# Output weights and residual rows of a dilated-attention layer prepared ahead, in the stage of the values

## The chip, the cores and the metric

One of the eight cores of a Trainium2 chip runs the kernel. The metric is the device time of one execution in microseconds (us); the time of a version is the median of its runs. Engines are named as the profile names them: PE (TensorE), DVE (VectorE), ACT (ScalarE), POOL (GpSimd) and SP (SyncE), whose queue issues most transfers.

## The reference

Two post-norm layers over x of 1024 rows by 1024 columns, in f32. Each sub-layer is modulated by a conditioning vector c, and its residual is scaled by ALPHA:

```python
for i in range(DEPTH):                       # DEPTH = 2
    shift, scale, gate = ada_mod(c, ada_w[i, 0], ada_b[i, 0])
    h = x * (1.0 + scale) + shift
    y = mixer_a(h, ...) if i % 2 == 0 else mixer_b(h, b_w_qkv, b_w_out, slopes)
    x = layer_norm(ALPHA * x + gate * y, ln_g[i, 0], ln_b[i, 0])
    shift, scale, gate = ada_mod(c, ada_w[i, 1], ada_b[i, 1])
    h = x * (1.0 + scale) + shift
    y = squared_relu_mlp(h, mlp_w_up[i], mlp_w_down[i])
    x = layer_norm(ALPHA * x + gate * y, ln_g[i, 1], ln_b[i, 1])
```

The change lies in `mixer_b`, the attention of the second layer. h times `b_w_qkv` gives query, key and value of 16 heads for each of three patterns (dilation 1, 4 and 16). Each pattern attends within its window, the three outputs are weighted by the softmax of their log-sum-exps and added, and the sum (1024 by 1024) is multiplied by `b_w_out`. The result, times `gate`, is added to ALPHA times the normalised rows of the sub-layer before, which are (z - mean) * rstd * ln_g + ln_b.

## The kernel before

Every f32 product is made of three products of rounded halves: a tensor is split into `hi` (a cast, on ACT) and `lo` (the rest, on DVE), and hi*hi, hi*lo and lo*hi are summed in PSUM. `split` (lines 102 and 103) is the helper for it, so that nearly all splits have these two lines; the tile's name tells them apart. Stages follow one another: `mixer_a` (gMLP), `mlp(1)`, `values`, `attention` with its tail `go_on`, `mlp(3)`. Tile pools give buffers by tag; an instruction that writes a buffer again waits for its last reader. A scheduler orders each engine's instructions when the kernel is built, except those pinned by `keep_in_program_order`.

**`values`** (line 1131 on) makes the values of the three patterns and the queries and keys of the first. A 1024 by 1024 by 1024 product is done by seven products of half-size blocks instead of eight (a Strassen scheme); `V_STEPS` lists five such groups of seven steps, numbered p = 1, 2, 5, 6, 7, 4, 3. A step (a block product) is four row blocks m of 12 matmuls, 48 in all. While step n runs, its loop loads the raw right-hand blocks of step n+2 (`vraw`, `v_r`, `v_t`, from SP), splits those of step n+1 into `vrhi` and `vrlo`, and evicts its own sums: p = 1, 5 and 6 by a copy on ACT (`vpart`), the others by an addition and a split into `vs` or `qs`, which a DMA of POOL's queue stores to DRAM. Some steps continue a sum in the PSUM bank of an earlier one (1, 6, 7, 4 in one, 2 and 5, 3 in others), so an eviction has to be done before the bank's next step. The left-hand forms are built on the way by a generator (`stream`); the four tiles `l21` are held until the last group, where they are split again (`place("L21", ...)`).

**`attention`** works through 24 groups, eight head pairs `hp` of three patterns g each. `order` and `slots` lay its steps out by hand: a group has eight slots of two halves, and `at(slot, half)` puts a step there. Meanwhile `project()` makes queries and keys of the other patterns, and fills PE between the small matmuls of the groups. Per group `scores` and `soften` give the probabilities `p`, `transposes` turns them (`pT`), `halve` splits them (`pThi`, `pTlo`), `weighted` multiplies them with the values (`pv`, line 1527), and `gather` copies the sum (`oT`, lines 1536 and 1537). `merge` joins the three patterns of a pair: it reads the statistics (`mst`), computes weights (`ma`), writes them to DRAM (`w_dram`), reads them back spread over all rows (`bc`, line 1611), scales `oT` by them (line 1623), adds (line 1627) and cuts the result (`oTs`, or `o_dram` for the first six pairs). Its twelve steps begin 18 half-slots after the pair's base.

Two more jobs lie in the slots. The **residual rows**: the affine part of the layer norm before (times ln_g, plus ln_b, both scaled by ALPHA) is applied to the eight row blocks of `spill[1]`, in slots 0 to 23 (`affine_load`, `affine_row`, line 1678); the first output rows add them by a DMA. The **output weights**: `staged_unit` loads 128 rows of `b_w_out` (`wo_raw`), multiplies them by the gate (line 1712) and splits them (`wo_hi`, `wo_lo`): units 0 to 3 from 14 slots before the last group on, 4 and 5 within it, 6 and 7 at its end and in `go_on`. `accumulate` (line 1756) makes the output product from them in five parts, named in the sums: `psoa`, `psob` between the last groups, then, behind the last `pv`, `psoc`, `psod` and `psoe` in `go_on` and beside the start of `mlp(3)`.

Of the kernel before, what the change touches and what calls it, by code (L numbers as in the profile page):

```python
# [10 lines left out]
F32 = mybir.dt.float32  # L11
# [24 lines left out]
def trunk(ctx: ExitStack, tc: tile.TileContext, x, c, ada_w, ada_b, ln_g, ln_b, a_w_in, a_b_in,  # L36
# [165 lines left out]
    def run(gen):  # L202
        for _ in gen:
            pass
# [867 lines left out]
    v_dram = [dram.tile([S, N_PAIRS, 4 * HEAD], F32, name=f"v_{g}") for g in range(3)]  # L1072

    qk_dram = dram.tile([N_PAIRS, 2, P, 2, S], F32, name="qk_0")

    class RightForms:
        BLOCK = {1: (0, 0), 2: (1, 0), 5: (0, 1), 6: (1, 1), 7: (0, 1), 4: (1, 0)}
# [53 lines left out]
    def values(before, right, ahead):  # L1131
# [3 lines left out]
        with ExitStack() as ph:  # L1135
# [12 lines left out]
            def x_tile(nm):  # L1148
                return xp.tile([P, HALF], F32, name=nm, tag="x")

            l21 = [hold.tile([P, HALF], F32, name=f"l21_{k}") for k in range(4)]

            def h_row(k, dst):
                pst = bank("tr", f"pst_2_0_{k}")
# [18 lines left out]
            def second():  # L1173

                for f in ("L22", "S1"):
                    form[f] = form_tile(f)
                for f in ("S2", "S3"):
                    form[f] = form_tile(f, act2)
                form["S4"] = form_tile("S4", top)
                x22 = []  # L1180
                for k in range(4):
                    h_row(k, l21[k][:])
# [3 lines left out]
                    V.tensor_tensor(s1[:], l21[k][:], x22[k][:], op=ALU.add)  # L1186
                    place("S1", k, s1[:])
                    yield
                trs.close()
                open_psum(trs, "VX", pbx=2)  # L1190
                built.add("S1")
                for k in range(4):
                    s3 = x_tile(f"s3_{k}")
                    sub(s3[:], form["L11"][:, 0, k, :], l21[k][:])
                    plus_lo("L11", k, s3[:])
                    place("L22", k, x22[k][:])
                    sub(x22[k][:], x22[k][:], s3[:])
                    place("S2", k, x22[k][:])
                    yield
                    place("S3", k, s3[:])  # L1200
                    yield
                built.add("S2")
                built.update(("S3", "L22"))
                for k in range(4):
                    s4 = x22[k]
                    sub(s4[:], form["L12"][:, 0, k, :], s4[:])
# [8 lines left out]
            def evict(g, X, p, m):  # L1215
# [10 lines left out]
                if X < 2:  # L1226
# [7 lines left out]
                nc.gpsimd.dma_start(v_dram[g][i * P : (i + 1) * P, 4 * dh : 4 * dh + 4, :],  # L1234
                                  v[:].rearrange("p h f c -> p h (f c)").bitcast(F32))

            for n, (g, X, p) in enumerate(V_STEPS):
                while name[p] not in built:
                    next(stream)
                for m in range(4):  # L1240
                    if m % 2 == 0 and n + 1 < len(V_STEPS):
                        right.prepare(*V_STEPS[n + 1], m // 2)
                    if m % 2 and n + 2 < len(V_STEPS):
                        right.load(*V_STEPS[n + 2], m // 2)
                    if p in (1, 2, 5):
                        kind = "pa" if p == 1 else "pbx" if m > 1 and n > 1 else "pb"
                        sums["pa" if p == 1 else "pb", m] = bank(kind, f"psv{p}_{g}_{X}_{m}")
                    acc = sums["pb" if p in (2, 5, 3) else "pa", m][:]
                    left = form[name[p]]
                    for kp in range(2):  # L1250
                        r = right.ready[g, X, p, kp]
                        for k in range(2):
                            for a, b in TERMS:
                                rows, cols_ = left[:, a, 2 * kp + k], r[b][:, k]
                                if X < 2:
                                    rows, cols_ = r[a][:, k], left[:, b, 2 * kp + k]
                                T.matmul(acc, rows[:, m * P : (m + 1) * P], cols_,  # L1257
                                         start=p in (1, 2, 5) and kp + k + a + b == 0,
                                         stop=kp == 1 and k == 1 and a == 1, skip_group_check=True)
# [12 lines left out]
    def attention(form):  # L1272
# [5 lines left out]
        with ExitStack() as ph:  # L1278
# [290 lines left out]
            def merge(hp, oTs):  # L1569
# [74 lines left out]
                steps = [lambda f=f, g=g, half=half: f(g, half) for f, g in pieces for half in range(2)]  # L1644
                pace = 2 if hp < N_PAIRS - 2 else 1
                for n, f in enumerate(steps):
                    n = pace * n + 18
                    at(base + n // 2, n % 2)(f)

            for hp in range(N_PAIRS):  # L1650
# [7 lines left out]
                merge(hp, oTs)  # L1658


            affine = {}

            def affine_load(i):
                if i == 0:
                    for n, src in (("g", ln_g), ("b", ln_b)):
                        affine[n] = row_bc(f"aff_{n}")
                        nc.sync.dma_start(affine[n][:], src[0, 1].partition_broadcast(P))
                t = affine[i] = vec.tile([P, S], F32, name=f"aff_{i}", tag="oT", bufs=4) if i < 4 else row_bc(f"aff_{i}")
                nc.sync.dma_start(t[:], spill[1][i * P : (i + 1) * P, :])

            def affine_scale():
                for n in "gb":
                    A.mul(affine[n][:], affine[n][:], ALPHA)

            def affine_row(i):
                t = affine[i]
                for n, op in (("g", ALU.mult), ("b", ALU.add)):
                    tc.keep_in_program_order(V.tensor_tensor(t[:], t[:], affine[n][:], op=op))
                nc.gpsimd.dma_start(spill[1][i * P : (i + 1) * P, :], t[:])

            at(0, 0)(affine_scale)
            for i in range(NT):
                if i > 3:
                    at(5 * i - 15, 0)(lambda i=i: affine_load(i))
                at(*((i + 1, 1) if i < 4 else (5 * i - 12, 1)))(lambda i=i: affine_row(i))
# [7 lines left out]
            def pinned_split(hi, lo, src):  # L1693
                for x_ in split(hi, lo, src):
                    tc.keep_in_program_order(x_)

            @at(last_group - 13, 0)
            def gate_row():
                ending["gate"] = vec.tile([P, D], F32, name="gate_2", tag="oT", bufs=4)
                nc.sync.dma_start(ending["gate"][:], gate_dram[2].partition_broadcast(P))  # L1700

            def staged_unit(k, load, gate, ready):
                box = {}

                @at(last_group + load[0], load[1])
                def load_raw():
                    box["raw"] = wts.tile([P, D], F32, name=f"wo_{k}_raw", tag="raw", bufs=2)
                    nc.sync.dma_start(box["raw"][:], b_w_out[0, k * P : (k + 1) * P, :])

                @at(last_group + gate[0], gate[1])  # L1710
                def apply_gate():
                    tc.keep_in_program_order(V.tensor_tensor(box["raw"][:], box["raw"][:], ending["gate"][:], op=ALU.mult))

                def split_raw():
                    hi, lo = (wts.tile([P, D], F32R, name=f"wo_{k}_{m}", tag=f"w{m}")[:] for m in ("hi", "lo"))
                    pinned_split(hi, lo, box["raw"][:])
                    ending["units"][k] = hi, lo

                if ready is None:
                    return split_raw  # L1720
                at(last_group + ready[0], ready[1])(split_raw)

            staged_unit(0, (-14, 0), (-12, 0), (-11, 0))
            staged_unit(1, (-13, 0), (-11, 1), (-10, 1))
            staged_unit(2, (-11, 0), (-10, 0), (-9, 0))
            staged_unit(3, (-10, 1), (-9, 1), (-8, 0))
            staged_unit(4, (-2, 0), (2, 0), (8, 0))
            staged_unit(5, (-1, 0), (4, 0), (8, 1))
            late = [staged_unit(6, (9, 0), (11, 1), None), staged_unit(7, (9, 1), (12, 1), None)]

            @at(last_group - 9, 0)
            def rows_first():
# [45 lines left out]
            def go_on():  # L1778
                steps = ending["merge"]
                for n, _ in enumerate(accumulate(1, range(2, 4), name="c")):  # L1780
                    if n > 4:
                        steps.pop(0)()
                for f in late:
                    f()
# [13 lines left out]
            lead, credit = 7 * KD, 0  # L1798
            for n in range(lead):
                next(stream)  # L1800
                if 16 <= n < 20:
                    affine_load(n - 16)
            due = 0
            for n, slot in enumerate(slots):
                for half, pos in enumerate(slot):
# [52 lines left out]
```

## Time and profile before

| what | us |
|---|---|
| median of 3 runs (lowest to highest) | 2732.57 (2730.59 to 2736.09) |
| the profiled execution, its own time | 2727.96 |
| its span in the profile | 2726.2 |
| `values`, in the span | 991 to 1377 |
| `attention` to the last `pv` | 1377 to 2033 |
| `psoc`, `psod`, `psoe` | 2033 to 2096 |
| `mlp(3)`, the rest | 2096 to 2726 |

Times in the profile count from the start of the span. A row of a group reads: line, engine, operation, output <- inputs, shapes and count | busy time in us, mean of one in ns | idle time of the engine just before it, and what ended most of it. A row of a wait reads: who waited <- for whom: us in total, times, the longest. A row of the timeline begins with its start and length in us.

### The profile page before, as it was taken

Reading aid. Unit: us, or ns where it says so; the run is one execution under the profiler, and the core shown is the slowest. Engines: PE = TensorE matmul, PEld = TensorE weight load, DVE = VectorE, ACT = ScalarE, POOL = GpSimd, SP = SyncE. Lnnn points to the kernel's source line nnn. Section 1 sums busy time; section 2 is a strip of 40 time slices with the busy share of each in tenths; the row PEclk is TensorE's granted clock in tenths of the full one; section 3 lists DMA queues with packets and bytes.
Section 4 is the critical chain, followed back from the end, with each engine's and each line's share of the span. In section 5 each row is a group of like instructions: output and inputs, shape, how many; then the busy total and the mean of one; then the engine's idle time right before and its main releaser. Section 6 shows DMA issues by size and latency. Waiting matters only on the chain.

```text
span 2726.2 us, 36911 instructions
## 1 busy us (share of the span) xinstructions
PE 2658.8 (98%) x13242; PEld 2196.3 (81%) x13242; DVE 1989.8 (73%) x3594; ACT 1377.1 (51%) x2593; POOL 97.0 (4%) x161
## 2 busy tenths in 40 slices
PE   6999999999999999999999999999999999999998
PEld 5788888887888878888888888888777788878886
DVE  6787698787867778555557767777768966577877
ACT  3354375555443464434436666666655655554332
POOL 1000000000000000111110000000010000000000
PEclk9999999999999999999999999999999999999999
DMA  7534346667936545655565554555672654485562
GB/s 263 159 118 134 116 140 224 227 214 257 333 131 194 195 155 193 212 186 182 178 210 153 155 140 129 132 144 139 193 183 105 202 189 159 149 311 192 171 207 86
DMA packets 332572, 487.98 MB, mean 179 GB/s; under 512 B 50988, under 2 KB 176340, under 8 KB 332388
## 3 DMA queue, kind: packets, MB, share of 16 engines
q1 hardware_dynamic: 318564, 435.29, 50.3%
q0 software_dynamic: 13824, 50.34, 5.2%
q8 instruction: 104, 1.70, 0.3%
q14 instruction: 80, 0.66, 0.1%
HBM read 357.01 MB, written 128.53 MB: 178 GB/s over the span
## 4 chain that ended last, share of the span: by engine, by line
PE 77%; DVE 12%; DMA 6%; ACT 3%; issue 2%; SPq 1%; DVEq 0%; ACTq 0%
PE psd L955 22%; PE psv L1257 13%; PE psua L796 7%; PE psq L1358 6%; PE psk L1358 6%; DMA adaw<-in_ada_w_dram 3%; PE psuc L796 3%; PE psd_wout L389 3%; PE psu L368 3%; PE pv L1527 3%; PE sc L1447 2%; PE psv L470 2%; PE psub L796 2%; DVE adaacc L128 1%; DVE left L103 1%
## 5 line engine op out<-in xcount | busy, mean ns | idle before, releaser
L796 PE MATMUL psua<-right,left 128*128 128x512 f32 x1536 | 363.4, 390 | 0.3
L955 PE MATMUL psd<-rhi,lhi 128*128 128x512 f32 x896 | 349.9, 390 | 3.0 <-ACT part L827 3.0
L955 PE MATMUL psd<-rlo,lhi 128*128 128x512 f32 x896 | 349.6, 390 | 0.2
L955 PE MATMUL psd<-rhi,llo 128*128 128x512 f32 x896 | 349.2, 390 | 0.0
L796 PEld LDWEIGHTS psua<-right,left 128*128 128x128 f32 x1536 | 287.1, 188 | 61.7 <-DVE right L103 1.4
L1469 ACT ACTIVATE p<-p,stat 128x128 f32<-128x128 f32 (+1 forms) x384 | 168.7, 441 | 107.8 <-DVE stat L1467 104.7
L955 PEld LDWEIGHTS psd<-rhi,lhi 128*128 128x128 f32 x896 | 168.6, 188 | 39.1 <-ACT part L827 3.9
L955 PEld LDWEIGHTS psd<-rlo,lhi 128*128 128x128 f32 x896 | 168.5, 188 | 35.9 <-DVE rlo L103 1.1
L955 PEld LDWEIGHTS psd<-rhi,llo 128*128 128x128 f32 x896 | 168.6, 188 | 35.0
L796 PE MATMUL psuc<-right,left 128*128 128x512 f32 x768 | 187.2, 390 | 0.0
L128 DVE SCALAR_TENSOR_TENSOR adaacc<-adaw,silu_c,adaacc 128x512 f32<-128x512 f32 x168 | 128.5, 775 | 55.0 <-DMA adaw<-in_ada_w_dram 54.6
L796 PEld LDWEIGHTS psuc<-right,left 128*128 128x128 f32 x768 | 143.5, 188 | 30.0 <-DVE right L103 0.4
L103 DVE TENSOR_TENSOR pTlo<-pT,pThi 128x512 fp32r<-128x512 f32 (+1 forms) x160 | 99.3, 621 | 75.1 <-ACT pThi L102 74.1
L103 DVE TENSOR_TENSOR left<-ws,left 128x512 fp32r<-128x512 f32 x128 | 87.8, 688 | 71.5 <-ACT left L102 69.7
L103 DVE TENSOR_TENSOR llo<-lraw,lhi 128x1024 fp32r<-128x1024 f32 x112 | 136.4, 1218 | 0.8 <-ACT lhi L102 0.8
L102 ACT CAST left<-ws 128x512 fp32r<-128x512 f32 x128 | 79.1, 620 | 99.1 <-DVE ws L717 87.8
L1358 PE MATMUL psk<-form_L,wqk_hi 128*128 128x512 f32 x384 | 127.0, 412 | 0.0
L1358 PE MATMUL psq<-form_L,wqk_hi 128*128 128x512 f32 x384 | 126.4, 410 | 0.0
L102 ACT CAST rhi<-rraw 128x1024 fp32r<-128x1024 f32 x48 | 50.6, 1053 | 139.6 <-issue 113.7
L1257 PE MATMUL psv<-vrhi,form_S 128*128 128x512 f32 x384 | 119.9, 390 | 0.6 <-ACT vrhi L102 0.4
L102 ACT CAST lhi<-lraw 128x1024 fp32r<-128x1024 f32 x112 | 117.4, 1048 | 3.5 <-PE psua L796 3.5
L1467 DVE CUSTOM_DVE_ANT_0 p<-sc,bias 128x128 f32<-128x128 f32 (+1 forms) x384 | 113.6, 346 | 6.7 <-PE sc L1447 5.8
(326 smaller groups left out, 6094.4 us busy)
## 6 DMA issues: line engine op xcount, KB each, us to landing
lraw<-forms SPq DMA_DIRECT2D x112, 512.0 KB
adaw<-in_ada_w_dram SPq DMA_DIRECT2D x192, 256.0 KB
up<-in_mlp_w_up_dram SPq DMA_DIRECT2D x64, 512.0 KB
forms<-s SPq DMA_DIRECT2D x128, 256.0 KB
rraw<-in_mlp_w_down_dram SPq DMA_DIRECT2D x64, 512.0 KB
forms<-part SPq DMA_DIRECT2D x96, 256.0 KB
v<-vs POOLq DMA_DIRECT2D x48, 512.0 KB, 3.7
vraw<-in_b_w_qkv_dram SPq DMA_DIRECT2D x42, 512.0 KB
```

The source lines that it names most:

```text
L102: first = A.copy(hi, src) if hi_engine is A else hi_engine.tensor_copy(hi, src)
L103: return first, lo_engine.tensor_tensor(lo, src, hi, op=ALU.subtract)
L128: ins = V.scalar_tensor_tensor(acc[:], raw[:], silu_c[:, k : k + 1], acc[:], ALU.mult, ALU.add)
L368: T.matmul(dst, s[a], m[b], start=(n == 0), stop=(n == last))
L389: T.matmul(p[:], stat[a][:, k, o : o + P], u[b][:, w], start=n == 0, stop=n == count - 1)
L796: T.matmul(acc, w[:, a, k, :], right[p][:, b, k, :], start=p in (1, 2, 5) and k + a + b == 0, stop=k == 3 and a == 1, skip_group_check=True)
L955: ins = T.matmul(sums[kind, m][:], l[a][:, k, m * P : (m + 1) * P], r[b][:, k, :], start=p in (1, 5, 2, 3) and kp + k + a + b == 0, stop=k ...
L1257: T.matmul(acc, rows[:, m * P : (m + 1) * P], cols_, start=p in (1, 2, 5) and kp + k + a + b == 0, stop=kp == 1 and k == 1 and a == 1, ski ...
L1358: T.matmul(p[:], wu[a][:, k * P : (k + 1) * P], h_op(k, half, b), start=k + c_ == 0, stop=k == KD - 1 and c_ == 2)
L1467: V.tensor_tensor_reduce(out=pr, in0=banks[e][:, sl], in1=st["bias"][:, width - w :], scale=-0.125, scalar=3e38, op0=ALU.add, op1=ALU.min, ...
L1469: A.activation(pr, pr, AF.Exp, bias=nm, scale=-1.0, accum_out=l)
L1527: T.matmul(pvs[b][:, q0 % HALF : q0 % HALF + w_], stt, x_[:, o_ : o_ + w_], start=not begun[b], stop=left[b] == 0, skip_group_check=True)
```

## The change

Both jobs move into `values`, as 24 pieces. The four `l21` tiles become two tiles of twice the size under one tag (`side`, two buffers); once the forms are built they are stored to DRAM by POOL (`x21_dram`), and the two buffers serve the pieces. From the sixth step on, each step begins one piece (its load, from SP) and carries out the one before it: sixteen weight pieces (half a unit each: load, times gate, split, store to `wo_dram`) and eight row pieces (256 rows of half the columns: load, times g, plus b, store back to `spill[1]`). No piece begins in the first four steps of the last group, in which `l21` is read back into the two buffers. In `attention` both jobs go; a unit is now two loads of 512 KB, hi and lo, each issued where a tile comes free: unit 3 into the two `raw` tiles, units 0, 1, 2 and 4 into `whi` and `wlo` behind the last project units, 7 into a tile of the values, 5 and 6 behind units 0 and 1. The twelve steps of a merge begin 22 half-slots after the base instead of 18.

```diff
-            l21 = [hold.tile([P, HALF], F32, name=f"l21_{k}") for k in range(4)]
+            side = [hold.tile([P, 2, HALF], F32, name=f"l21_{k}", tag="side", bufs=2) for k in range(2)]
+            l21 = [side[k // 2][:, k % 2, :] for k in range(4)]
...
+                for k in range(2):
+                    nc.gpsimd.dma_start(x21_dram[k], side[k][:])
                 built.add("S2")
...
+            def row_halves(*srcs):
+                across.clear()
+                for src in srcs:
+                    across.append(work.tile([P, HALF], F32, name=f"row_{len(across)}", tag="h"))
+                    nc.sync.dma_start(across[-1][:], src.partition_broadcast(P))
+
+            def weight_piece(k, dh):
+                if k + dh == 0:
+                    row_halves(gate_dram[2, 0:HALF], gate_dram[2, HALF:])
+                t = side_tile(f"wo_{k}_{dh}")
+                nc.sync.dma_start(t[:, 1], b_w_out[0, k * P : (k + 1) * P, dh * HALF : (dh + 1) * HALF])
+                yield
+                V.tensor_tensor(t[:, 1], t[:, 1], across[dh][:], op=ALU.mult)
+                split(t[:, 0].bitcast(F32R), t[:, 1].bitcast(F32R), t[:, 1])
+                nc.gpsimd.dma_start(wo_dram[k, :, dh, :, :], t[:])
+
+            def row_piece(i, dh):
+                w = slice(dh * HALF, (dh + 1) * HALF)
+                if i == 0:
+                    row_halves(ln_g[0, 1, w], ln_b[0, 1, w])
+                t = side_tile(f"aff_{i}_{dh}")
+                src = spill[1][2 * i * P : 2 * (i + 1) * P, w].rearrange("(n p) c -> p n c", p=P)
+                nc.sync.dma_start(t[:], src)
+                yield
+                if i == 0:
+                    for r in across:
+                        A.mul(r[:], r[:], ALPHA)
+                for n in range(2):
+                    V.tensor_tensor(t[:, n], t[:, n], across[0][:], op=ALU.mult)
+                    V.tensor_tensor(t[:, n], t[:, n], across[1][:], op=ALU.add)
+                nc.gpsimd.dma_start(src, t[:])
+
+            pieces = deque([weight_piece(k, dh) for k in range(N_PAIRS) for dh in range(2)] + [row_piece(i, dh) for dh in range(2) for i in range(4)])
...
                     evict(g, X, p, m)
+                    if n > 4 and m == 0:
+                        for _ in range(len(begun)):
+                            next(begun.popleft(), None)
+                        if pieces and n not in (28, 29, 30, 31):
+                            begun.append(pieces.popleft())
+                            next(begun[-1])
...
-                        place("L21", m, l21[m][:])
+                        place("L21", m, back[m // 2][:, m % 2, :])
+                    if (g, X) == V_STEPS[-1][:2] and p == 2 and m < 2:
+                        back.append(side_tile(f"back_{m}"))
+                        nc.sync.dma_start(back[m][:], x21_dram[m])
...
-                    n = pace * n + 18
+                    n = pace * n + 22
...
-            affine = {}
...
-            staged_unit(0, (-14, 0), (-12, 0), (-11, 0))
...
+            def load_unit(k):
+                if k == 7:
+                    t = qp.tile([P, 2, D], F32R, name="wo_7", tag="v")
+                    ending["units"][k] = tuple(t[:, i, :] for i in range(2))
+                else:
+                    ending["units"][k] = tuple(wts.tile([P, D], F32R, name=f"wo_{k}_{m}", tag="raw" if k == 3 else f"w{m}", bufs=2 if k == 3 else 4)[:] for m in ("hi", "lo"))
+                for i, t in enumerate(ending["units"][k]):
+                    nc.sync.dma_start(t.rearrange("p (d c) -> p d c", c=HALF).bitcast(F32), wo_dram[k, :, :, i, :])
+
+            for k, half_slot in ((3, -34), (0, -32), (1, -30), (2, -27), (4, -15), (7, 11), (5, 17), (6, 18)):
+                in_half(2 * last_group + half_slot, 4)(lambda k=k: load_unit(k))
```

More of the change, by code (lines that the diff above doesn't have):

```diff
@@ L1074, in trunk @@
     qk_dram = dram.tile([N_PAIRS, 2, P, 2, S], F32, name="qk_0")
+    wo_dram = dram.tile([N_PAIRS, P, 2, 2, HALF], F32, name="wo_parts")
+    x21_dram = dram.tile([2, P, 2, HALF], F32, name="x21")
     class RightForms:
@@ L1181, in second @@
                 for k in range(4):
-                    h_row(k, l21[k][:])
+                    h_row(k, l21[k])
                     x22.append(x_tile(f"l22_{k}"))
@@ L1185, in second @@
                     s1 = work.tile([P, HALF], F32, name=f"s1_{k}", tag="h")
-                    V.tensor_tensor(s1[:], l21[k][:], x22[k][:], op=ALU.add)
+                    V.tensor_tensor(s1[:], l21[k], x22[k][:], op=ALU.add)
                     place("S1", k, s1[:])
@@ L1193, in second @@
                     s3 = x_tile(f"s3_{k}")
-                    sub(s3[:], form["L11"][:, 0, k, :], l21[k][:])
+                    sub(s3[:], form["L11"][:, 0, k, :], l21[k])
                     plus_lo("L11", k, s3[:])
@@ L1235, in evict, with side_tile @@
                                   v[:].rearrange("p h f c -> p h (f c)").bitcast(F32))
+            back, across, begun = [], [], deque()
+            def side_tile(nm):
+                return hold.tile([P, 2, HALF], F32, name=nm, tag="side", bufs=2)
+            def row_halves(*srcs):
[28 more added lines that the diff above has]
+            pieces = deque([weight_piece(k, dh) for k in range(N_PAIRS) for dh in range(2)] + [row_piece(i, dh) for dh in range(2) for i in range(4)])
             for n, (g, X, p) in enumerate(V_STEPS):
+                if n == 5:
+                    run(stream)
                 while name[p] not in built:
@@ L1658, in attention @@
                 merge(hp, oTs)
-            affine = {}
[L1663 to L1685, printed above, removed]
             last_group = 8 * (len(order) - 1)
@@ L1691, in attention @@
             done = ending["res"] = Residual(2)
[L1693 to L1721, printed above, removed]
@@ L1723, in attention @@
-            staged_unit(0, (-14, 0), (-12, 0), (-11, 0))
[L1724 to L1729, printed above, removed]
+            def load_unit(k):
[6 more added lines that the diff above has]
+                    nc.sync.dma_start(t.rearrange("p (d c) -> p d c", c=HALF).bitcast(F32), wo_dram[k, :, :, i, :])
@@ L1782, in go_on @@
                         steps.pop(0)()
-                for f in late:
-                    f()
                 for f in steps:
@@ L1800, in attention @@
                 next(stream)
-                if 16 <= n < 20:
-                    affine_load(n - 16)
             due = 0
```

## The prediction

> **What bounds the kernel now.** I read the page's head first, then a table of stretches cut by stage, then who PE and VectorE waited for, and last the instructions of VectorE and PE in the one stretch that is bad.
>
> ```profile
> span 2726.2 us, 36911 instructions
> PE 2658.8 (98%) x13242; PEld 2196.3 (81%) x13242; DVE 1989.8 (73%) x3594; ACT 1377.1 (51%) x2593; POOL 97.0 (4%) x161
> ```
>
> PE is busy almost throughout, so an edit on another engine pays only where PE stands idle or runs at a reduced clock. The table of stretches says where that is (the number behind POOL's is the granted clock, then come the DMA share and GB/s).
>
> ```profile
> core 0: us, PE busy (x) PEld busy (x) DVE busy (x) ACT busy (x) POOL busy (x), PEclk, DMA share, GB/s
> 991.00:1377.00 386.00, 385.36 (x1714) 318.24 (x1713) 248.09 (x311) 171.65 (x244) 47.83 (x80) 1.00 0.57 197
> 1410.00:1500.00 90.00, 89.88 (x601) 75.01 (x600) 64.82 (x175) 54.28 (x161) 9.84 (x13) 1.00 0.48 141
> 1500.00:1700.00 200.00, 196.96 (x1316) 164.50 (x1315) 142.54 (x444) 126.30 (x379) 5.95 (x16) 1.00 0.53 142
> 1700.00:1950.00 250.00, 249.98 (x1702) 211.20 (x1703) 175.44 (x559) 159.34 (x480) 7.24 (x20) 1.00 0.52 142
> 1950.00:1960.00 10.00, 9.51 (x66) 7.98 (x64) 8.48 (x21) 6.68 (x18) 0.81 (x2) 1.00 0.75 219
> 1960.00:1970.00 10.00, 6.25 (x47) 5.30 (x46) 7.00 (x22) 5.41 (x20) 0.00 (x0) 0.96 1.00 308
> 1970.00:1980.00 10.00, 7.35 (x44) 5.53 (x42) 10.00 (x16) 4.60 (x9) 0.00 (x0) 0.84 0.76 244
> 1980.00:1990.00 10.00, 10.00 (x43) 8.29 (x43) 5.09 (x18) 6.67 (x20) 2.50 (x4) 0.85 1.06 269
> 2020.00:2030.00 10.00, 8.84 (x59) 7.60 (x58) 6.55 (x18) 7.21 (x13) 1.71 (x2) 1.00 0.64 103
> 2030.00:2040.00 10.00, 8.96 (x29) 7.20 (x30) 8.01 (x13) 1.52 (x3) 0.00 (x0) 0.66 0.71 189
> ```
>
> The first row is the values stage, into which the change moves work: PE idles 0.64 us of 386, VectorE has 138 us free, DMA runs at 0.57. The second is the start of attention, out of which the residual rows are taken: PE idles 0.12 us there. Idle PE lies at 1500 to 1700 (3.04 us), 1950 to 1980 (0.49 + 3.75 + 2.65 = 6.89 us) and 2020 to 2040 (1.16 + 1.04 = 2.20 us). Besides that the clock falls: ten microseconds at 0.96, 0.84, 0.85 and 0.66 are 0.4 + 1.6 + 1.5 + 3.4 = 6.9 us of lost time, all behind those two idle stretches. What PE waited for, from 1410 to 1950 and then from 1950 to 2040:
>
> ```profile
> PE pv L1527 <- DVE pTlo L103: 2.7, 4, 1.2
> PE pv L1527 <- ACT pThi L102: 0.3, 1, 0.3
> ...
> PE pv L1527 <- DVE pTlo L103: 4.9, 6, 2.3
> PE pv L1527 <- ACT pThi L102: 3.7, 2, 3.3
> ```
>
> It is always the split of a transposed probability tile, so VectorE (or ScalarE behind it) was late. Of VectorE's own waits in 1410 to 1950 one group matters, and the timeline shows the bad stretch:
>
> ```profile
> DVE bc L1623 <- DMA bc<-w_dram: 14.2, 5, 3.7
> ...
> 1963.92 1.98 DVE L1623 TENSOR_TENSOR bc<-oT,bc 128x512 f32<-128x512 f32 x2 [1.97 <-DMA bc<-w_dram]
> 1969.09 1.21 DVE L1712 TENSOR_TENSOR wo_raw<-wo_raw,gate 128x1024 f32<-128x1024 f32 x1
> 1978.70 1.21 DVE L103 TENSOR_TENSOR wo_lo<-wo_raw,wo_hi 128x1024 fp32r<-128x1024 f32 x1
> ...
> 1967.71 0.33 PE L1527 MATMUL pv<-pThi,v 128*128 128x128 f32 x1 [3.26 <-ACT pThi L102]
> 1978.22 0.33 PE L1527 MATMUL pv<-pTlo,v 128*128 128x128 f32 x1 [2.27 <-DVE pTlo L103]
> ```
>
> VectorE takes its queue in order. The merge's scaling (L1623) waits for the spread weights `bc` to land, and the splits behind it wait too; then gate products and splits of the output weights, 1.2 us each, stand before the next splits.
>
> **The change part by part.** Removed from attention:
>
> ```profile
> L1712 DVE TENSOR_TENSOR wo_raw<-wo_raw,gate 128x1024 f32<-128x1024 f32 x8 | 9.7, 1218 | 0.7 <-DMA wo_raw<-in_b_w_out_dram 0.6
> L103 DVE TENSOR_TENSOR wo_lo<-wo_raw,wo_hi 128x1024 fp32r<-128x1024 f32 x8 | 9.6, 1215 | 0.5 <-ACT wo_hi L102 0.4
> L1678 DVE TENSOR_TENSOR aff<-aff,aff_b 128x1024 f32<-128x1024 f32 x8 | 9.9, 1240 | 0.2
> L1678 DVE TENSOR_TENSOR aff<-aff,aff_g 128x1024 f32<-128x1024 f32 x8 | 9.8, 1219 | 0.0
> ```
>
> *Residual rows* (16 x 1.23 = 19.7 us of VectorE at 1410 to 1500). PE idles 0.12 us there: gain 0.
>
> *Merge steps two slots later* (18 to 22 half-slots). Some 200 slots lie between the first scores and the first product that follows the last group:
>
> ```profile
> 1415.29 1.48 PE sc L1447 x24
> ...
> 2032.97 13.16 PE psoc L1756 x48
> ```
>
> A slot is thus 3.1 us (estimate), and the scaling comes 6.2 us later. The longest wait for `bc` is 3.7 us, so every one ends before the scaling asks. PE's waits in this stretch are 3.0 us, not all of them behind `bc`: gain 2.5 us (0 to 3.0). Late next are the end of the merge and the store of its rows, which are read only in the output product.
>
> *Gate products and splits* (16 x 1.22 = 19.4 us of VectorE). The same two groups in 1950 to 1980 alone:
>
> ```profile
> L1712 DVE TENSOR_TENSOR wo_raw<-wo_raw,gate 128x1024 f32<-128x1024 f32 x4 | 4.9, 1213 | 0.0
> L103 DVE TENSOR_TENSOR wo_lo<-wo_raw,wo_hi 128x1024 fp32r<-128x1024 f32 x4 | 4.8, 1210 | 0.4 <-ACT wo_hi L102 0.4
> ```
>
> That is 9.7 us where VectorE is full. With them and the wait for `bc` gone, of the 6.89 us I take 6.0 (bounds 3 and 6.9): the merge of the seventh head pair still falls into this stretch, though 6 us later, where VectorE was half idle (5.09 of 10). The two dips of the clock behind it go as well: 3.5 us (0 to 3.5).
>
> The Trainium skill (TensorE: Matmul & The Clock Gate, Part 1) says that the clock is halved after an idle window of about 3.4 us and given back after a busy one. The largest single gap here, 3.26 us, agrees, but the later dips follow gaps of 2.27 us and less, so by that rule taken strictly only the first dip (0.4 + 1.6 = 2.0 us at most) would go with the gap, and the sum would be 3.2 us smaller. The measured windows decide.
>
> *Last group*, 2020 to 2040. Two splits of output weights stand in front of the last probability splits:
>
> ```profile
> 2030.33 1.22 DVE L103 TENSOR_TENSOR wo_lo<-wo_raw,wo_hi 128x1024 fp32r<-128x1024 f32 x1
> 2030.47 0.39 PE L1527 MATMUL pv<-pTlo,v 128*128 128x256 f32 x1 [0.95 <-DVE pTlo L103]
> ```
>
> They go, but this stretch is also a bare chain of transpose, split, product with nothing to fill it, so I take half: 1.1 of 2.2 us idle, 1.7 of 3.4 us clock (bounds 0 and 5.6).
>
> *Unit loads.* Sixteen loads of 512 KB replace eight and the gate row: about 4 MB more on SP's queue. Each waits for its tile (last project units, then the second half's first product). Queued behind them are `mst`, `w_dram` and `bc` of the last two merges. Units 0 to 3 go out before the tail, as tiles come free, where DMA stands at 0.52; cost 0, up to the whole 6.9 us if `bc` is pushed behind them (second rival).
>
> **What the values stage pays.** Its rows for 512 columns, a block product, and the transfers:
>
> ```profile
> L1223 DVE TENSOR_TENSOR vpart<-psv,vpart 128x512 f32<-128x512 f32 x60 | 41.1, 685 | 6.3 <-PE psv L1257 6.3
> L103 DVE TENSOR_TENSOR vs<-vpart,vs 128x512 fp32r<-128x512 f32 x36 | 24.8, 688 | 11.0 <-ACT vs L102 11.0
> L102 ACT CAST vs<-vpart 128x512 fp32r<-128x512 f32 x36 | 22.4, 621 | 55.7 <-DVE vpart L1223 28.5 <-DMA v<-vs 19.0 <-DVE vraw L1110 4.6
> ...
> 1377.21 10.88 PE psq L1358 x48
> 2155.67 4.18 DMA adaw<-in_ada_w_dram
> ...
> adaw<-in_ada_w_dram SPq DMA_DIRECT2D x192, 256.0 KB
> v<-vs POOLq DMA_DIRECT2D x48, 512.0 KB, 3.7
> ```
>
> Sixteen weight pieces cost VectorE 16 x (0.685 + 0.688) = 22.0 us, eight row pieces 8 x 4 x 0.685 = 21.9 us: 44 us into 138 us free. Over 29 products of 48 matmuls (10.88 us) that is 1.5 us a product. DMA gets 16 x 0.75 MB + 8 x 1 MB = 20 MB over 316 us, 63 GB/s on 197; the row at 1960 shows 308 GB/s at share 1.00, so it fits on average. Raw blocks for the products and the stores of `v` share the two queues with the pieces: SP waits for a side tile's store before it can issue a piece's load, and raw blocks stand behind.
>
> In the built order VectorE gets about six weight pieces between the last split for product 6 and the third eviction of product 7, three turns of each tile, with PE-critical splits between them. A turn by rows is load 4.18 + 0.685 + 0.621 + 0.688 + store 3.7 = 9.9 us, perhaps 10.5 with hand-overs (estimate). From product 5's middle to the point where product 4 needs that eviction's bank are 3.1 products, 34 us: three turns of 10.5 just fit. I take 2.5 us of PE idle for the stage. Bounds: not below -0.6 (PE idles no more than that now), and 44 us were all of it on the path; I stay near the lower end because an eviction's bank is asked for one product less one block later, 10.88 - 2.72 = 8.2 us.
>
> The Trainium skill (DMA: Bandwidth & Descriptors, Anatomy of one DMA) gives 2.0 us plus bytes over 436 KB per us; that makes 2.6 us for the load and 3.2 us for the store, an estimated turn of 7.8 us, by which the stage would pay nothing and the sum would be 2.5 us better. The store's row is 3.7 us, so I keep the rows.
>
> **Sum.** 2.5 + 6.0 + 3.5 + 1.1 + 1.7 - 2.5 = 12.3 us less. The profiled execution took 2727.96 us (span 2726.2 and 1.8 around it), 4.6 us under the median of the runs; I take the difference from the median: 2732.6 - 12.3 = 2720.3 us.
>
> **Rivals.**
>
> *The two tiles turn too slowly (slower than before).* In the values stage a VectorE instruction of a piece waits for a load that waits for a store, and splits and evictions wait behind it. For: the queue order above, and ScalarE already waits 19.0 us for stores of `v` in the row quoted. Against: the 8.2 us of cover. It decides from a turn of about 12.4 us, where 3 x (3 x 1.1 + 1.7) is 15. Three turns fit until 34 / 3 = 11.3 us. At 13.5 us they overrun by 6.6 us in each of the three groups of products that take pieces, and each such idle stretch brings a dip of 1.7 us as above: 3 x 8.3 = 25 us against 14.8 gained, about 2743 us.
>
> *The wait for `bc` stays* (no measurable change). With 4 MB more in flight at a share near 1.00, the last two spreads land later by as much as the merge was put back. Then 1950 to 1990 keep their idle time and dips, and only the early merges and the last group gain: 2.5 + 2.8 - 2.5 = 2.8 us, about 2730 us. Against: loads leave early.
>
> *The work removed was not what held PE*: the splits are late because of ScalarE (3.7 of the 8.6 us are laid at `pThi`). Then half of 1950 to 1980 remains: half of its dips too: 12.3 - 3.0 - 1.8 = 7.5 us, about 2725 us, still faster.
>
> **How the numbers follow.** Differences under 0.2% (5.5 us) can't be told from none. Forecast with its weaker form (third rival): 0.68, all faster. `bc` stays: 0.13, same. Slow turn: 0.19, slower. Low end: all bounds, 3.0 + 6.9 + 3.5 + 5.6 = 19.0 us, and 1.5 of scatter give 2712. High end: 2737, which takes in the second rival and the milder part of the first, and leaves out its worse part.
>
> **What would show it.** Right: PE idle of under 1.5 us and the clock at 1.00 in the stretches that answer to 1950 to 1990; no wait of VectorE for `bc` in the early merges; the values stage at 386 to 390 us with PE idle of 1 to 4 us. Wrong: PE waits for `vrlo`, `vrhi` or `vpart` in the values stage of over 8 us with dips of the clock there; or `bc` still ending VectorE's idle time before L1623's successor, with DMA near 1.00; or the dip after the last group unchanged.

## The result, and the profile after

The changed kernel takes **2751.09 us** (median of 6 runs, 2749.04 to 2757.96) against 2730.99 us for the kernel before (6 runs, 2725.82 to 2736.09): a ratio of 1.0079, 95% interval 1.0062 to 1.0095. It is 20 us slower where 12 us less had been forecast. The head of the profile after:

```profile
span 2749.1 us, 37080 instructions
PE 2664.9 (97%) x13242; PEld 2198.7 (80%) x13242; DVE 1993.0 (72%) x3626; ACT 1377.2 (50%) x2603; POOL 105.2 (4%) x179
```

VectorE's work is what it was (1989.8 us before), and PE's, for the same number of products, has grown by 6 us, so most of the difference is waiting. Stage by stage, from the starts of TensorE's first and last products of each stage in the two traces:

| stretch | before | after | difference |
|---|---|---|---|
| values, first to last `psv` | 385.6 | 417.0 | +31.4 |
| first `sc` to first `psoc` | 617.5 | 610.9 | -6.6 |
| `psoc` to the first product of the next MLP | 62.9 | 61.0 | -1.9 |
| from there to the end | 620.0 | 620.2 | +0.2 |

What the change was to win behind the values stage is there, at 8.5 us instead of 14.8. The whole loss is in the values stage. The table of stretches after (time, then busy time of PE, PEld, DVE, ACT, POOL, then the granted clock, the DMA share and GB/s):

```profile
991.00:1409.00 418.00, 395.98 (x1717) 322.99 (x1716) 287.69 (x377) 179.67 (x263) 63.43 (x106) 0.98 0.67 234
1047.00:1124.00 77.00, 71.20 (x304) 58.39 (x303) 54.41 (x69) 31.68 (x48) 12.81 (x24) 0.96 0.81 281
1124.00:1200.00 76.00, 66.89 (x279) 53.93 (x278) 53.62 (x70) 31.01 (x47) 13.05 (x24) 0.96 0.79 276
1200.00:1280.00 80.00, 73.62 (x313) 59.19 (x312) 52.44 (x68) 27.22 (x39) 12.08 (x20) 0.98 0.74 257
```

From 1047 to 1280, while pieces are prepared, PE idles 5.80 + 9.11 + 6.38 = 21.3 us, and the lower clock costs 0.04 x 77 + 0.04 x 76 + 0.02 x 80 = 7.7 us: 29.0 of the 31.4 us. What PE and VectorE waited for from 1040 to 1280 (total, times, longest):

```profile
PE psv L1303 <- DVE vpart L1228: 14.7, 4, 5.8
PE psv L1303 <- DVE vrlo L103: 3.8, 1, 3.8
PE psv L1303 <- ACT vpart L1224: 2.9, 2, 1.8
...
DVE wo L1259 <- DMA wo<-in_b_w_out_dram: 23.5, 6, 6.6
...
DVE aff L1275 <- DMA aff<-spill: 14.0, 5, 6.3
DVE aff L1275 <- ACT row L1273: 5.0, 1, 5.0
```

PE waits for the evictions and splits of its own products; VectorE, which makes them, waits 42.5 us at the first instruction of a piece (L1259, L1275): 37.5 us for a load that has not landed and 5.0 us for ScalarE's scaling of the row halves. One such stall in the timeline after, first VectorE, then SP, POOL, ScalarE and PE (start, duration, and in brackets the idle time before it and its releaser):

```profile
1086.06 0.69 DVE L1259 TENSOR_TENSOR wo<-wo,row 128x512 f32<-128x512 f32 x1 [1.12 <-DMA wo<-in_b_w_out_dram]
...
1095.76 0.69 DVE L1259 TENSOR_TENSOR wo<-wo,row 128x512 f32<-128x512 f32 x1 [6.63 <-DMA wo<-in_b_w_out_dram]
1096.37 1.22 DVE L103 TENSOR_TENSOR vrlo<-v_t,vrhi 128x1024 fp32r<-128x1024 f32 x1
...
1099.90 0.68 DVE L1228 TENSOR_TENSOR vpart<-psv,vpart 128x512 f32<-128x512 f32 x1
...
1081.03 0.34 SPq L1257 DMA_DIRECT2D wo<-in_b_w_out_dram  x1
...
1091.14 3.29 SPq L1257 DMA_DIRECT2D wo<-in_b_w_out_dram  x2
...
1082.36 0.53 POOL L1261 DMA_DIRECT2D wo_parts<-wo  x1 [1.21 <-DVE wo L103]
...
1088.89 0.54 POOL L1261 DMA_DIRECT2D wo_parts<-wo  x1 [3.02 <-DVE wo L103]
...
1088.78 1.06 ACT L102 CAST vrhi<-v_t 128x1024 fp32r<-128x1024 f32 x1
1090.21 1.07 ACT L102 CAST vrhi<-v_t 128x1024 fp32r<-128x1024 f32 x1
...
1100.73 0.76 PE L1303 MATMUL psv<-vrhi,form_S 128*128 128x512 f32 x1 [5.80 <-DVE vpart L1228]
```

The multiply that began at 1095.76 had stood at the head of VectorE's queue for 6.63 us, since 1089.13. Its load went out only at 1091.14, 8.8 us after the store of the same tile (1082.36), on which SP waited. Behind the multiply stood two splits `vrlo`, whose casts had ended at 1089.84 and 1091.28, and the addition `vpart` that frees a bank, for which PE stopped for 5.8 us.

### The profile page after: what moved, and what is told of

Same layout as the page of the kernel before. It is cut to its first block, busy times and chain, and to the rows that moved or that the text cites. A ratio compares the mean times of both kernels' runs of the same rounds, so it can differ in the third digit from the quotient of the medians.

```text
span 2749.1 us, 37080 instructions
## 1 busy us (share of the span) xinstructions
PE 2664.9 (97%) x13242; PEld 2198.7 (80%) x13242; DVE 1993.0 (72%) x3626; ACT 1377.2 (50%) x2603; POOL 105.2 (4%) x179
## 4 chain that ended last, share of the span: by engine, by line
PE 70%; DVE 11%; issue 7%; DMA 7%; ACT 3%; POOL 1%; SPq 1%; DVEq 0%; POOLq 0%; ACTq 0%
PE psd L955 22%; PE psua L796 7%; PE psv L1303 6%; PE psq L1413 6%; PE psk L1413 6%; DMA adaw<-in_ada_w_dram 3%; PE psuc L796 3%; PE psd_wout L389 3%; PE psu L368 3%; PE pv L1582 3%; PE sc L1502 2%; DVE adaacc L128 1%; PE psub L796 1%; DVE left L103 1%; PE psv L470 1%
```

## The experiments

Three theories were told apart. *Queue order*: the built order puts a piece's instruction that waits for a transfer too early in an in-order queue, and what PE needs stands behind it. *Traffic*: 20 MB more delay the stage's own transfers. *DVE time*: 44 us more work is too much. Every kernel was timed beside the kernel before on the same chip, and the ratio to that is given with its interval.

### The pieces held in program order, and the kernel without pieces

**no_pieces** leaves the preparation out: `pieces = deque()`, and the units are loaded from `qk_dram[k, 0, :, i, :]`, which has the same size. The kernels with transfers alone, arithmetic alone and without pieces below load them from there too.

> The changed kernel without its pieces in the values stage: the output weights and residual rows are not prepared, and the units are loaded from pairs of the queries' rows instead (same bytes). If the 31.5 us of the values stage come from the pieces by whichever way (all theories), the stage is 385 to 387 us again as before, and what is left is the gain behind it: the attention stage 6.7 us shorter as in the changed kernel's trace, the rest 2 us, so 2722 us. If instead the late values stage also spoiled the attention stage (loads that still ran, a clock that had dipped), the forecast's 14.8 us appear and the time is 2714 us.

2718.97 us, ratio 0.9963 (0.9951 to 0.9975), between the two times written down. The values stage is 386.1 us, the first `sc` to `psoc` 611.8. Without the pieces the values stage is what it was, and the gain behind it stays: it does not depend on how late that stage ends.

**pinned**: the two tiles, transfers and instructions of the change, with each piece's arithmetic ordered behind what the code issues before it on its engine.

```diff
-                V.tensor_tensor(t[:, 1], t[:, 1], across[dh][:], op=ALU.mult)
-                split(t[:, 0].bitcast(F32R), t[:, 1].bitcast(F32R), t[:, 1])
+                tc.keep_in_program_order(V.tensor_tensor(t[:, 1], t[:, 1], across[dh][:], op=ALU.mult))
+                for x_ in split(t[:, 0].bitcast(F32R), t[:, 1].bitcast(F32R), t[:, 1]):
+                    tc.keep_in_program_order(x_)
...  (the row pieces' four instructions alike)
```

> The changed kernel with each piece's multiply, split and row arithmetic held behind what the code issues ahead of it on its engine, so that a piece's first DVE instruction can't stand in the queue before the products ahead of it. Same work, same transfers, same two tiles. Theory queue order (a piece's DVE instruction is queued many places too early, waits for its load, and the splits and sums that PE needs stand behind it): the values stage returns to 386 to 392 us and the time to 2720 to 2728 us. Theory traffic (the 20 MB more that the stage moves delay its own loads and stores) and theory DVE time (the work itself is too much): the stage stays at 410 to 417 us and the time at 2745 to 2752 us.

2722.89 us, 0.9976 (0.9961 to 0.9991), the stage 388.8 us in the profile (its execution took 2731.41 us, the longest of ten, mostly by what it lost behind this stage). The group of the 16 multiplies, in the profile after and in that of this kernel (count, durations in ns, start of the first and the last):

```profile
L1259 DVE TENSOR_TENSOR wo<-wo,row x16: 679/684/693, 1059.2 to 1171.2; 128x512 f32<-128x512 f32 x16
```

```profile
L1259 DVE TENSOR_TENSOR wo<-wo,row x16: 681/684/687, 1074.9 to 1232.7; 128x512 f32<-128x512 f32 x16
```

The change's code begins a piece at every product of 10.9 us. As built, the multiplies come every 112.0 / 15 = 7.5 us, in bunches; held, every 157.8 / 15 = 10.5 us, so that each of the two tiles has 21 us for a turn, and none of them waits for its load. The stretches of the held kernel move nearly as many bytes as those of the change, and PE doesn't idle in them:

```profile
1047.00:1124.00 77.00, 77.00 (x342) 63.75 (x341) 56.64 (x70) 36.23 (x53) 11.75 (x22) 1.00 0.79 274
1124.00:1200.00 76.00, 76.00 (x337) 62.94 (x336) 52.28 (x65) 34.02 (x50) 12.29 (x23) 1.00 0.75 266
```

Neither the traffic nor the work explains the loss, and two tiles are enough.

**first_pinned**: of each piece only the first VectorE instruction is held.

> The changed kernel in which of each piece only the first DVE instruction (the one that waits for the load) is held behind what the code issues ahead of it; the split, the rest of the row arithmetic, the loads and the stores are placed freely, as in the changed kernel. Theory queue order: the place of the waiting instruction is what counts, so the values stage is 386 to 392 us and the time 2720 to 2727 us, as with all of them held. Rival (the places of the loads and stores in SP's and POOL's queues do the harm, as in the kernel with the transfers alone): the stage stays above 400 us and the time above 2738 us.

2727.95 us, 1.0001 (0.9992 to 1.0010), the stage 393.2 us: just past the upper end expected. Holding one instruction a piece takes back 23.8 of the 31.4 us. What is left is not at the weight pieces, whose multiplies don't wait. Half of PE's waits in the stage, 3.1 of 6.1 us, lie at the first row piece: its multiply, though held, waited for its load, and its addition, which was left free, stood on VectorE for ScalarE's scaling of the row halves.

```profile
1237.46 0.69 DVE L1275 TENSOR_TENSOR aff<-aff,row 128x512 f32<-128x512 f32 x1 [3.20 <-DMA aff<-spill]
1242.11 0.69 DVE L1278 TENSOR_TENSOR aff<-aff,row 128x512 f32<-128x512 f32 x1 [3.96 <-ACT row L1273]
```

### Transfers alone, and arithmetic alone

**transfers_only** stores each tile as it was loaded; **work_only** repeats the arithmetic on two tiles that stay.

> The changed kernel with the pieces' loads and stores, without their arithmetic (the tiles are stored as they were loaded; the units are loaded from pairs of the queries' rows). Theory traffic: the values stage stays near 410 us or above and the time at 2740 to 2752 us. Theory queue order on DVE, and theory DVE time: the stage is 386 to 390 us and the time 2721 to 2726 us. A middle result (395 to 405 us) would say that the loads and stores do harm by their places in the queues of SP and POOL.

> The changed kernel with the pieces' arithmetic on two tiles that stay where they are, without their loads (but the first two) and stores; units again from pairs of the queries' rows. Theory DVE time: the values stage stays above 405 us and the time at 2740 us or more. Theory queue order: nothing waits for a load any more, so the stage is 386 to 392 us and the time 2721 to 2728 us. Theory traffic: the same, 386 us and 2721 us.

`work_only` took 2722.95 us, 0.9972 (0.9957 to 0.9987), stage 389.2: DVE time falls. `transfers_only` took **2752.49 us**, 1.0086 (1.0060 to 1.0111), stage 420.4, as slow as the change although no piece touches VectorE. By what had been written that spoke for traffic. Its waits on POOL and ScalarE from 1047 to 1280 speak of something else:

```profile
POOL wo_parts L1262 <- DMA wo<-in_b_w_out_dram: 51.3, 14, 7.4
POOL spill L1272 <- DMA wo<-spill: 33.9, 7, 8.3
...
ACT vs L102 <- DMA v<-vs: 96.8, 26, 19.9
```

The pieces' stores now wait at the head of POOL's queue for their loads, 85 us in all, with the values' stores behind them; so the two staging tiles `vs` come free late, ScalarE waits for them up to 19.9 us, and the splits and copies behind that are what PE lacks. The same mechanism, in another queue. To tell it from traffic, **transfers_held** orders only those stores behind the stores that the code issues before them:

```diff
-                nc.gpsimd.dma_start(wo_dram[k, :, dh, :, :], t[:])
+                tc.keep_in_program_order(nc.gpsimd.dma_start(wo_dram[k, :, dh, :, :], t[:]))
...  (the rows' store alike)
```

> The kernel with the pieces' transfers alone (2752 us), with each piece's store held on POOL behind the stores that the code issues ahead of it. Theory queue order: the transfers cost nothing by themselves, and the 25 us came from stores that stood on POOL waiting for their loads, with the values' own stores behind them; the values stage is 386 to 390 us and the time 2719 to 2724 us. Theory traffic: the same bytes move, so the stage stays above 405 us and the time above 2740 us.

2717.46 us, 0.9972 (0.9963 to 0.9982), stage 386.9. The same bytes cost the stage 1 us. Traffic falls, and 33.5 us of the stage (420.4 against 386.9) hang on the place of 24 stores in one queue.

### The terms of the gain

**no_pieces_18** and **shift_only** take the merges' shift apart (`n = pace * n + 18` without pieces, `+ 22` in the kernel before); **rows_back** puts the residual rows back into the attention stage, without pieces.

> The kernel without pieces (2719 us, 10 us under the kernel before) with the merges' steps put back from 22 to 18. The forecast gave the shift 2.5 us (the early merges' waits for their factors): by it this run takes 2721.5 us, and PE's waits for the split p tiles near 104 and 179 us after the first score product come back at 0.9 and 1.3 us. If the 10 us come from the removed preparation alone, it stays at 2719 us.

> The kernel before with one number changed: the merges' steps at 22 instead of 18. The forecast's term: 2.5 us less, 2726 us. If the shift is worth nothing by itself: 2729 us. If the later steps collide with the last group's preparation, which still stands there: 2731 us or more.

> The kernel without pieces (2719 us), with the residual rows scaled in the attention stage again, by the code of the kernel before. The forecast gave the residual rows nothing: then this takes 2719 us as well, and all of the 10 us comes from the output weights' preparation and the shift. Rival: the rows' instructions on DVE in the attention stage held PE up by what the forecast's windows did not show: 2722 to 2725 us.

`no_pieces_18`: 2720.87 us, 0.9976 (0.9966 to 0.9986), 1.9 us above `no_pieces` by the medians, which are of two chips, and 3.5 by the ratios. `shift_only`: 2725.56 us against 2728.20, 0.9995 (0.9984 to 1.0007). Both agree with a shift worth some 2 us; neither shows it against no shift at all. Of the two waits of PE that were expected back in `no_pieces_18`, the one at 104 us came (0.88 us); the one at 179 us (1.21 us) is there with the shift and not without it. `rows_back`: 2718.82 us, 0.9975 (0.9966 to 0.9985). That is the median of `no_pieces`, but on another chip; the ratios lie 3 us apart, within their intervals. Where the rows stood, the traces have nothing for them to cost: in 90 us at the start of the attention stage PE idles 0.17 us with them and 0.12 us without.

### The last group, and a version that beats both

In the profile of the held kernel PE still stops 7 us in the last group. Its VectorE, SP and PE there:

```profile
2030.11 0.18 DVE L1646 TENSOR_TENSOR mm<-mst 128x16 f32<-128x16 f32 x1 [6.49 <-DMA mst<-st_dram]
...
2013.87 1.17 SPq L1729 DMA_DIRECT2D wo<-wo_parts  x2
2018.91 0.33 SPq L1616 DMA_DIRECT2D st_dram<-statT  x1
2024.13 0.36 SPq L1638 DMA_DIRECT2D mst<-st_dram  x1
...
2032.42 0.69 PE L1583 MATMUL pv<-pThi,v 128*128 128x256 f32 x2 [6.99 <-ACT pThi L102]
```

The last statistics (32 x 128 x 4 bytes, 16 KB) go out to DRAM and come back, with the megabyte of unit 7 ahead of them: 11.2 us from 2018.91 to 2030.11. This is the worst case on record: in the eight other profiles with unit 7 ahead the way out and back took 6.4 to 9.1 us, and VectorE waited 1.7 to 4.4 us. **pinned_late7** issues unit 7 behind the statistics' load, with the pieces held.

> The held pieces (2723 us), with the load of output unit 7 (1 MB) issued behind the last pair's statistics instead of ahead of them. Theory: in the last group DVE's first merge instruction waits for the statistics (6.5 us in the profile of the kernel with held pieces, 2.1 us without pieces), since their store and their load run beside that megabyte; ACT and PE stand behind it for 7 us. With the load behind, the wait is 1 to 2 us and the time 2717 to 2721 us. Rival: the three late units then run beside the factors' store and the broadcasts, which the last merge needs, and the wait only moves there: 2723 us or more.

2720.34 us, 0.9973 (0.9962 to 0.9984). VectorE's wait for the statistics is gone:

```profile
DVE bc L1681 <- DMA bc<-w_dram: 5.1, 1, 5.1
DVE mm L1648 <- DMA mst<-st_dram: 0.3, 1, 0.3
```

The rival was right in part: a wait for `bc` of 5.1 us now stands there, where the profile with unit 7 early has none (2.9 us in that of the change), and in the 60 us from the first `psoc` PE idles 3.8 us instead of 1.6. In the traces more was won than that: from the first `sc` to the first `psoc` it takes 605.2 us, and 605.5 and 606.7 in the two kernels below that also have unit 7 late, against 611.8 in `no_pieces` and 617.3 in the profile of the held kernel. The times do not show a gain: the 2.6 us between the medians are of two chips, and the ratios, 0.9976 and 0.9973, lie under 1 us apart. That the wait went is shown, that it pays is not. Last, the rows left where PE does not wait for them (**weights_held**: 16 weight pieces held, unit 7 late, the old code for the rows), and the kernel with all 24 pieces again beside it:

> The 16 weight pieces held as before, unit 7 behind the last statistics, and the residual rows left in the attention stage, where they cost nothing (2719 us with them there and no pieces, as without). Theory: the values stage, 2.6 us longer in the profile with all 24 pieces held, gets back at least a third of that, and nothing is paid elsewhere: 2716 to 2720 us, against 2720 us with all pieces held. Rival: the 2.6 us come from the weights' pieces, or the rows collide with the later merges' steps: 2720 to 2724 us.

> All 24 pieces held and unit 7 behind the last statistics, the same kernel as in the earlier run (2720 us), beside the kernel with the rows left in the attention stage: 2720 us again, 7 to 8 us under the kernel before.

`weights_held`: **2718.16 us**, 0.9961 (0.9947 to 0.9975), stage 386.6. `pinned_late7_again`: 2721.18 us, 0.9974 (0.9962 to 0.9985), stage 391.3 (388.2 in the profile of the earlier run). The version with the rows left alone has the lowest median of those that compute all, some 11 us under the kernel before and, by the ratios, 32 us under the change as made; its lead over the one with all pieces is inside the intervals.

## Why the prediction was wrong

**The values stage (forecast 2.5 us, measured 31.4): the step that failed.** The working had found the cause, six weight pieces in VectorE's queue between two points that PE needs, and asked only whether three turns of a tile fit there. It took 10.5 us a turn and found no overrun, so it laid almost nothing at PE. The sign of being wrong that it had named, waits of over 8 us for `vrlo`, `vrhi` or `vpart` with dips, came with 21.9 us. In the timeline above one turn of the other tile goes from the load at 1081.03 to that tile's next load, the second of the two that the line at 1091.14 joins and that ends at 1094.43: at 0.34 us for an issue it began at 1094.1, so **13.1 us**. Load to multiply (1086.06) took 5.0 us (the row used had 4.18), arithmetic to the store's issue (1088.89) 2.8, store to the next load 5.2 (the row used had 3.7; the profile after has a median of 5.0 for these stores). The tile that stalled PE had needed 8.8 us for the last part alone. Of the twelve turns among the weight pieces from the third on, from a load's issue to the next one into the same tile, the shortest took 10.6 us, the longest 24.5, with a median of 13.2; five were within 11.5. The long ones are not transfers alone: in the longest, 16.9 us lay between the load's issue and the multiply. Both rows came from stages with a mean DMA share of 0.57 or less, and the stage runs at 0.8 with the pieces. By the fit of the Trainium skill (DMA: Bandwidth & Descriptors, Anatomy of one DMA) the turn was an estimated 7.8 us. The Trainium skill gives that fit for transfers that GpSimd issues, which is the store and not the load; for the store it makes 3.2 us, and the trace disagrees with 5.0.

**The first rival was right**, and its point (12.4 us) and price (25 us for 13.5 us) were near what came: 29.0 us of idle time and clock (at 13.1 us a turn its own sum gives 3 x (3 x 1.8 + 1.7) = 21 us). With rows of a less loaded stage at its edge, it deserved more than its chance. But its name says too much: with the same two tiles and store times of 5.1 us the held kernels lose 3 to 6 us in the stage. What the runs show in place of the 2.5 us is the built order: the same work and the same bytes cost 31.4 us as built and 3.1 us held (388.8 against 385.6).

**The residual rows (0)**: right, by the traces of `rows_back` and `no_pieces`. **The shift (2.5)**: 1.4 to 3.5 us by medians and ratios, not shown against nothing. Not every wait for `bc` ended: in the profile without pieces VectorE has one left in 1410 to 1950, of 6.0 us, longer than any of the five before (3.7). A slip on which nothing hangs: 16 x 1.22 us is 19.5 and not 19.4.

**The idle time and the dips at 1950 to 1980 (6.0 and 3.5), and in the last group (1.1 and 1.7)**: the idle time was there to win, but not so much of it, and not by the weights alone. The stretches 1950 to 2000 and 2000 to 2040, first before, then without pieces (whose `psoc` begins 6.5 us earlier, so that the second row is not quite the same work):

```profile
1950.00:2000.00 50.00, 43.10 (x252) 35.34 (x251) 35.79 (x90) 28.60 (x80) 4.27 (x7) 0.93 0.86 239
2000.00:2040.00 40.00, 37.55 (x215) 30.81 (x214) 26.31 (x64) 23.51 (x55) 4.24 (x5) 0.91 0.69 147
```

```profile
1950.00:2000.00 50.00, 47.24 (x292) 39.05 (x291) 27.91 (x84) 27.17 (x81) 4.06 (x6) 0.93 0.86 244
2000.00:2040.00 40.00, 37.11 (x201) 31.04 (x201) 22.62 (x55) 17.04 (x40) 4.24 (x5) 0.96 0.83 196
```

In the first, idle time falls by 4.1 us and the clock stays at 0.93; in the second, idle time stays (2.45 and 2.89 us) and the clock gives 2.0 us. VectorE did get free (62.1 to 50.5 us busy in the two), but what is late next was not named: the loads of `v` (2.8 us of PE's waits without pieces; why they are late is open), and the statistics behind unit 7. The shift alone frees the same idle time, with the weights still prepared there and VectorE as busy as before; this is the stretch of `shift_only` that answers to 1950 to 2000:

```profile
1948.00:1998.00 50.00, 47.29 (x267) 38.62 (x266) 35.43 (x83) 27.93 (x73) 3.90 (x5) 0.90 0.89 251
```

PE idles 2.71 us there instead of 6.90, and 2.87 us in `no_pieces_18`, which has the preparation removed and the shift not. For this idle time either step was enough, so their gains do not add as the sum had them. With the shift alone a lower clock (0.90 here, 0.87 in the 40 us behind, against 0.93 and 0.91 before) took part of it back. **The unit loads (0)** were wrong in one place. The forecast's bound had looked at `bc`, and it was mainly `mst` that was pushed behind them. In all, the gain behind the values stage was 10 us (0.9963, so 7 to 13), not 14.8. That is also what the third rival left behind that stage (7.5 + 2.5), by luck: its cause, a late ScalarE, is not the one seen.

## What to carry to other kernels

When work with a load and a store of its own goes into a stage with cover to spare, ask of each queue it enters where its waiting instruction will stand, and count the turn from rows taken at the load that the stage will then have. If a scheduler decides that place, read it from the built order and hold the waiting instruction, on whichever queue it waits (here VectorE's multiply, or POOL's store), behind the work that the bottleneck needs. Here free engine time and free bandwidth did not help while one early wait stopped an in-order queue.

## What was not expected of the hardware

The same 20 MB cost the values stage 33.5 us more or less by the order of issue alone, at a DMA share of 0.74 to 0.80 and 265 to 283 GB/s in the kernel that lost 1 us by them. The round trip of the 16 KB of statistics through DRAM, from the issue of its store to the instruction that reads it, took 6.4 to 11.2 us behind a megabyte (nine profiles), 5.0 us with the megabyte behind it (2012.47 to 2017.45), and 4.6 us in the kernel before (2020.72 to 2025.36).

The clock dips of the values stage were of one kind. From the starts of PE's matmuls in the profile after, the gaps of 4.0, 4.2, 4.3 and 6.2 us were each followed by 2.6 to 4.7 us at half the rate of matmuls, those of 2.1, 1.8 and 1.5 us by none. The rule of the Trainium skill (TensorE: Matmul & The Clock Gate, Part 1) that the prediction weighed, an idle window of about 3.4 us, agrees with these. Elsewhere it does not: the dip at 1980 before followed a wait of 2.27 us, and the stretch of `shift_only` above ran at 0.90 though PE's longest wait in it was 1.7 us.
